# Two more pauses for the recurrence of a hybrid encoder layer, behind its wide sums and before its state

## The chip, the cores and the metric

The kernel runs on one core of a Trainium2 chip. A core has five engines with instruction queues of their own: TensorE (PE in the profile, its weight loads PEld), VectorE (DVE), ScalarE (ACT), GpSimd (POOL) and SyncE (SP), and sixteen DMA engines that serve all of them. The metric is the device time in microseconds of one execution; lower is better.

## The reference

One layer of an encoder for 512 positions of width 1024, in float32. It has three parts, each between two RMS norms and added to the residual:

```python
h = rmsnorm(x, pre_mix_g[l])
aq, ak, av, hq, hf_fwd, hf_bwd, hi, hg = split_columns(h @ w_in[l], IN_SPLITS)
...
att = axial_gqa_attention(apply_rope(aq, cos, sin), apply_rope(ak, cos, sin), av)
rec = hgrn2_group(hq, hf_fwd, hf_bwd, hi, hg, lb_all[:, l], hg_out_norm_g[l])
mixed = jnp.concatenate([att, rec], axis=-1) @ w_out[l]
x = x + rmsnorm(mixed, post_mix_g[l])
...
x = x + rmsnorm(memory_cross_attention(h, m, w_xq[l], w_xkv[l], w_xo[l]), post_x_g[l])
...
x = x + rmsnorm(conv_ffn(h, w_up[l], conv_w[l], conv_b[l], w_down[l]), post_ffn_g[l])
```

The attention has 8 heads of 64 with 2 key heads. The recurrence (`rec`) is a gated scan in both directions with 4 heads of 128: a state of keys by values decays by a gate at each position and takes in the new key and value. The cross-attention reads 256 memory rows, and the feed-forward part has 2816 columns.

## The kernel before

Every large product is made of three matmuls on split operands: each float32 operand is a rounded high part and a remainder, and `mm3` (lines 296 to 298) adds high by high, high by low and low by high in PSUM. Weights come in units of 128 x 1024 through `issue`: a load to `raw` on the SP queue, a cast to `wh` on ScalarE (L240), and the remainder `wl`, for some units by VectorE (L242), for others as a negated copy (L245 on GpSimd, L247 on ScalarE) to which a DMA of the GpSimd queue adds the weight (L248). `issue_ahead` starts units up to three ahead of their use (`AHEAD`).

The order of the instructions comes about in two steps. First, Python generators write the program: each stream of work is a generator that yields how many microseconds of work it has just written, and `weave` goes on with the stream that has the least of its total behind it. The sum of these steps is the planner's clock (`clock[0]`), which is a plan and not a time. `pace(us)` lets a stream yield nothing until the other streams have moved that clock on by `us`. A stream in `late` that pauses is put level with the next one, so that it does not catch up afterwards. Second, the framework's scheduler orders each engine's queue: of the instructions that its model holds to be ready, the one written first goes first. An instruction written later can so still run earlier, where an engine has nothing else.

The first weave runs two streams: `mix_projections` (total 100; the projections of the output gate, of the heads 1 to 3 of the recurrence, of the queries, keys and values) and `all_cores` (share 53, `CORE_SHARE`; the heads of the recurrence, one after another). A projection step is six matmuls of 512 columns and 1.296 of the planner's clock. The weave ends with the projections. The second weave takes what is left of the recurrence (share 34), `attention` (46; 32 steps and 3 to finish, 1.1 each) and `attention_filler` (52). The filler holds eight products for the memory's keys (half as wide, on PSUM bank `b`), four units for the first half of the memory's values, and the first half of the output product, `res_first`, whose order of weights is 0, 2, 3, 1: it starts when all four heads of the recurrence are written. Attention starts, after `ATT_LEAD`, when the keys are turned and the fourth head has begun (`begun[0] < 4`).

One head, `hgrn_core`, computes the scan without a loop over positions: products of gated keys and queries within pairs of blocks of 1, 2, 4, up to 64 positions fill the matrix `diag` by masks, level 128 fills its neighbour, and a state of keys by values carries between the halves of the sequence. In the heads 0 to 2 (`wide`) the first level is made in another way: two element products `near`, split into `sides`, are summed over the keys by a matrix of ones and zeros (`parity`, L722, "the wide sums"), and the result is copied to `diag` on ScalarE (L723). Then each level has two products in place on VectorE (L711), a copy of keys on ScalarE (L682), eight records of matmuls on bank `c` (L685) and a copy by mask on VectorE (L725). At the end the keys are turned on TensorE (L697), copied on ScalarE (L698), multiplied with the values into the state (L702, copied at L704), and the output follows (L731 to L733), with its norm, gate, a last turn (L749) and a split.

Before the change a wide head pauses at two places: `CORE_WIDE` (8.0) ahead of the wide sums, so that VectorE can make `sides`, and `CORE_END` (4.5) ahead of the gate.

In attention a step writes scores (L921, bank `s`), the softmax (reduction L899, exponent L902, reciprocal L903, scaling L907 on ScalarE or L909 on VectorE), and, two steps later, four turns (L931, bank `o`) with a split (L139 on ScalarE, L140 on VectorE); every fourth step also weighs the values (L942).

Of the kernel before, what the change touches and what calls it, by code (L numbers as in the profile page):

```python
# [47 lines left out]
NEG_SCALAR = frozenset(range(9, 33))  # L48
NEG_POOL = frozenset(range(33, 42))
CORE_SHARE, ATT_LEAD = 53.0, 4.0  # L50
CORE_WIDE, CORE_END = 8.0, 4.5
KEY_TURNS = {1: (0, 1), 2: (2, 3)}
WARM, SPREAD_STEP = 4, 2
LEVELS = (1, 2, 4, 8, 16, 32, 64)
# [5 lines left out]
def pat(t, off, dims):  # L60
    a = t[:]
    return bass.AP(tensor=a.tensor, offset=a.offset + off, ap=[list(a.ap[0])] + [list(d) for d in dims])
# [14 lines left out]
def pace(us):  # L77
    end = clock[0] + us
    while clock[0] < end and not stuck[0]:
        yield None  # L80
# [27 lines left out]
def layer(tc, io, out):  # L108
# [14 lines left out]
    def small():  # L123
        return sm.tile([P, 16], F32, name="small", tag="small")

    def bank(tag):
        return ps.tile([P, 512], F32, name="ps_" + tag, tag=tag)

    def big(shape, dt=F32):
        return b8.tile(shape, dt, name="big", tag="big")  # L130

    def tmp2(shape=(P, 512), dt=F32, tag="ta"):
        return t2.tile(list(shape), dt, name="tmp2", tag=tag, bufs=TMP_BUFS[tag])
# [4 lines left out]
    def split(hi, lo, src, eng=None):  # L138
        nc.scalar.copy(hi, src)  # L139
        (eng or nc.vector).tensor_sub(lo, src, hi.bitcast(F32))  # L140
# [159 lines left out]
    def blk(b):  # L300
        return slice(b * P, (b + 1) * P)
# [338 lines left out]
    def hgrn_core(h):  # L640
        while h not in heads:
            yield None
        q, qk, tt = heads[h]
        begun[0] += 1
        room = big([P, 2048])
        a = room[:, 0:1024].rearrange("p (s w n) -> p s w n", s=NB, w=2)
        kt = room[:, 1024:1536].rearrange("p (s n) -> p s n", s=NB)
        st = room[:, 1536:1792].rearrange("p (g n) -> p g n", g=2)
        diag = a[:, :, 0, :]
        wide = h < 3  # L650
        near = room[:, 1024:2048]
        ksum = tmp2(tag="th")
        nc.scalar.mul(ksum, qk[:, 1, 0, :], oml[:, 0, h:h + 1])
        if wide:
            nc.vector.tensor_tensor(out=pat(near, T, [[2, T // 2], [1 - T, 2]]), in0=pat(qk, 0, [[2, T // 2], [T + 1, 2]]),
                                    in1=pat(qk, 3 * T + 1, [[2, T // 2], [-(T + 1), 2]]), op=ALU.mult)
        nc.vector.scalar_tensor_tensor(out=ksum, in0=qk[:, 1, 1, :], scalar=oml[:, 1, h:h + 1], in1=ksum,
                                       op0=ALU.mult, op1=ALU.add)
        if wide:
            pairs = lambda t: t.rearrange("p (i two) -> p i two", two=2)  # L660
            nc.vector.tensor_tensor(out=pat(near, 0, [[2, T // 2], [T + 1, 2]]), in0=pairs(ksum), in1=pairs(q),
                                    op=ALU.mult)
            sides = [[tmp2(dt=F32R, tag="th") for _ in range(2)] for _ in range(2)]
            for n in range(2):
                split(*sides[n], near[:, n * T:n * T + T])
        else:
            kc, qc = [tmp2(tag="th") for _ in range(2)]
            for side, to in ((1, kc), (0, qc)):
                nc.scalar.copy(to, pat(qk, side * 2 * T, [[2, T // 2], [T + 1, 2]]))
            o = bank("c").rearrange("p (b n) -> p b n", b=NB)  # L670
            for b in range(NB):
                nc.tensor.matmul(o[:, b, :], ksum[:, blk(b)], q[:, blk(b)], start=True, stop=True)
            nc.scalar.copy(diag, o)
            yield 1.0
        toff = 0
        for i, m in enumerate(LEVELS + (128, 256)):
            if m == 1 and wide:
                pass
            elif m <= 64:
                if m > 1:  # L680
                    kc = tmp2(tag="th")
                    nc.scalar.copy(kc, pat(qk, 2 * T, [[2 * m, T // (2 * m)], [T + m, 2], [1, m]]))  # L682
                o = bank("c").rearrange("p (b n) -> p b n", b=NB)
                for b in range(NB):
                    nc.tensor.matmul(o[:, b, :], kc[:, blk(b)], qc[:, blk(b)] if m == 1 else  # L685
                                     pat(qk, b * P, [[2 * m, P // (2 * m)], [T + m, 2], [1, m]]),
                                     start=True, stop=True)
            elif m == 128:
                o = bank("c").rearrange("p (b n) -> p b n", b=NB)
                for sb in range(NB):  # L690
                    tb = sb ^ 1
                    nc.tensor.matmul(o[:, sb, :], qk[:, 1, sb % 2, blk(sb)], qk[:, 0, tb % 2, blk(tb)],
                                     start=True, stop=True)
            else:
                o = bank("c").rearrange("p (b n) -> p b n", b=NB)
                for sb in range(NB):
                    nc.tensor.transpose(o[:, sb, :], qk[:, 1, sb // 2, blk(sb)], ident)  # L697
                nc.scalar.copy(kt, o)  # L698
                yield 0.5
                o = bank("c")[:, :256].rearrange("p (g n) -> p g n", g=2)  # L700
                for sb in range(NB):
                    nc.tensor.matmul(o[:, sb // 2, :], kt[:, sb, :], v[:, sb, blk(h)],  # L702
                                     start=sb % 2 == 0, stop=sb % 2 == 1)
                nc.scalar.copy(st, o)  # L704
                yield 1.0
                break
            nblk = T // m
            npair = nblk // 2
            for s, off, gap in ((1, 1, nblk - 1), (0, nblk + 1, -(nblk + 1))):
                c = pat(qk, s * 2 * T, [[2 * m, npair], [T + m, 2], [1, m]])  # L710
                nc.vector.tensor_tensor(out=c, in0=c, in1=pat(tt, toff + off, [[2, npair], [gap, 2], [0, m]]),  # L711
                                        op=ALU.mult)
            if m < 128:
                src = tt[:, toff:toff + 2 * nblk].rearrange("p (i two) -> p two i", two=2)
                toff += 2 * nblk
                nc.vector.tensor_mul(tt[:, toff:toff + nblk], src[:, 0, :], src[:, 1, :])
                if m == 1 and wide:
                    yield from pace(CORE_WIDE)
                    o = bank("c")
                    for n in range(2):  # L720
                        for k in range(2):
                            nc.tensor.matmul(o, parity[:, n:n + P], sides[n][k], start=n + k == 0, stop=n + k == 2)  # L722
                    nc.scalar.copy(diag, o.rearrange("p (b n) -> p b n", b=NB))  # L723
                else:
                    nc.vector.copy_predicated(diag, masks[:, i:i + 1, :].to_broadcast([P, NB, P]), o)  # L725
            else:
                nc.scalar.copy(a[:, :, 1, :], o)
            yield 1.0
        o = bank("c").rearrange("p (b n) -> p b n", b=NB)
        for tb in range(NB):  # L730
            nc.tensor.matmul(o[:, tb, :], a[:, tb, 0, :], v[:, tb, blk(h)], start=True, stop=False)  # L731
            nc.tensor.matmul(o[:, tb, :], a[:, tb ^ 1, 1, :], v[:, tb ^ 1, blk(h)], start=False, stop=False)
            nc.tensor.matmul(o[:, tb, :], qk[:, 0, tb // 2, blk(tb)], st[:, 1 - tb // 2, :], start=False, stop=True)  # L733
        on = tmp2((P, NB, P), tag="th")
        ss = small()
        for b in range(NB):
            nc.scalar.activation(on[:, b, :], o[:, b, :], ACT.Square, accum_out=ss[:, b:b + 1])
        r = rstd_of(ss[:, :NB], NB, P)
        yield 3.0
        if wide:  # L740
            yield from pace(CORE_END)
        while len(sg_box) < 1 + NB:
            yield None
        for b in range(NB):
            nc.vector.scalar_tensor_tensor(out=on[:, b, :], in0=o[:, b, :], scalar=r[:, b:b + 1],
                                           in1=sg_box[0][:, b, blk(h)], op0=ALU.mult, op1=ALU.mult)
        o = bank("c").rearrange("p (b n) -> p b n", b=NB)
        for b in range(NB):
            nc.tensor.transpose(o[:, b, :], on[:, b, :], ident)  # L749
        if h % 2 == 0:  # L750
            pair(mix, 2 + h // 2)
        split_scaled(*mix.get(4 + h, slice(0, T)), o.rearrange("p b n -> p (b n)"), og[:, 0:1])
        rec_done[0] += 1
        yield 0.5
# [643 lines left out]
```

## Time and profile before

| | |
|---|---|
| median of 3 runs | 814.44 us (814.04 to 815.73) |
| profiled execution | 814.31 us, its span 812.5 us |
| mean granted TensorE clock | 0.998 |
| busy: TensorE, weight loads | 800.7 us, 688.4 us |
| busy: VectorE, ScalarE, GpSimd | 582.7, 482.0, 136.5 us |
| first and last wide sums (L722) | 55.8 and 168.3 us |
| first and last scores of attention (L921) | 208.5 and 299.0 us |

Times of rows are microseconds from the first instruction. TensorE's records overlap, since its matmuls are pipelined, so a busy TensorE need not run at its peak; its idle time is what no record covers. In the table of stretches each line gives the bounds and length of a stretch and then, for each engine, its busy time in it with the count of instructions, the granted clock, and the mean busy share of the DMA engines with GB/s. In the list of waits each line names the instruction that waited, what ended the wait, the total, the count and the longest. In the list of groups each line gives line, engine, operation, output and inputs with shapes and count, then busy time, mean ns of one, and the engine's idle time ahead of them.

### The profile page before, as it was taken

What the parts mean: (1) busy time and instruction counts of PE and PEld (TensorE: products, weight loads), DVE (VectorE), ACT (ScalarE), POOL (GpSimd) and SP (SyncE); (2) the same over time, 40 slices, a digit from 0 to 9 for tenths busy, and PEclk for the clock granted to TensorE, in tenths of its full rate; (3) what the DMA queues carried; (4) which work ended last, traced back from release to release, by engine and by line L of the source; (5) the groups of instructions that cost most, each with busy time, mean ns of one, the idle gap of its engine ahead of it and who ended that gap; (6) DMA issues with size and microseconds to landing.
All of it is one profiled execution on the core that took longest, in us unless ns stands there. A gap on an engine that the chain in (4) does not pass through costs nothing.

```text
span 812.5 us, 11696 instructions
## 1 busy us (share of the span) xinstructions
PE 800.7 (99%) x4390; PEld 688.4 (85%) x4390; DVE 582.7 (72%) x878; ACT 482.0 (59%) x797; POOL 136.5 (17%) x213
## 2 busy tenths in 40 slices
PE   9999999999999999999999999999999999999996
PEld 7888878899988888888888898899999998888885
DVE  5467576698896765855453767987777788888765
ACT  6675774677978873645443553665555545566651
POOL 0111201334213102301011311211111111000301
PEclk9999999999999999999999999999999999999999
DMA  8596666679777752256634158776765667278842
GB/s 300 198 267 164 137 148 130 146 187 267 206 193 191 186 188 109 86 173 170 167 117 143 33 165 205 161 199 164 187 166 141 160 187 179 91 211 277 241 127 104
DMA packets 42458, 139.61 MB, mean 172 GB/s; under 512 B 5281, under 2 KB 6561, under 8 KB 42401
## 3 DMA queue, kind: packets, MB, share of 16 engines
q1 hardware_dynamic: 28944, 97.43, 35.0%
q0 software_dynamic: 12160, 38.54, 26.8%
q10 hardware_dynamic: 1296, 2.89, 1.0%
q8 instruction: 34, 0.56, 0.3%
q14 instruction: 24, 0.19, 0.1%
HBM read 135.17 MB, written 25.17 MB: 197 GB/s over the span
## 4 chain that ended last, share of the span: by engine, by line
PE 89%; DVE 4%; ACT 4%; issue 1%; DMA 1%; POOL 1%; SPq 0%; DVEq 0%; POOLq 0%
PE ps_b L298 9%; PE ps_b L297 9%; PE ps_b L296 9%; PE ps_s L296 7%; PE ps_s L298 7%; PE ps_s L297 7%; PE ps_o L296 5%; PE ps_o L298 5%; PE ps_o L297 5%; PE ps_c L296 4%; PE ps_c L298 4%; PE ps_c L297 4%; PE ps_c L685 2%; PE ps_o L942 1%; PE ps_o L931 1%; PE ps_s L921 1%
## 5 line engine op out<-in xcount | busy, mean ns | idle before, releaser
L240 ACT CAST wh<-raw 128x1024 fp32r<-128x1024 f32 x110 | 113.8, 1036 | 106.9 <-PE ps_b L297 30.2
L242 DVE TENSOR_TENSOR wl<-raw,wh 128x1024 fp32r<-128x1024 f32 (+1 forms) x77 | 92.9, 1209 | 72.5 <-ACT wh L240 72.4
L296 PE MATMUL ps_b<-big,wh 128*128 128x512 f32 (+1 forms) x344 | 122.2, 355 | 0.0
L298 PE MATMUL ps_b<-big,wl 128*128 128x512 f32 (+1 forms) x344 | 120.9, 351 | 0.0
L297 PE MATMUL ps_b<-big,wh 128*128 128x512 f32 (+1 forms) x344 | 120.4, 350 | 0.0
L298 PEld LDWEIGHTS ps_b<-big,wl 128*128 128x128 f32 x344 | 65.0, 189 | 8.7
L297 PEld LDWEIGHTS ps_b<-big,wh 128*128 128x128 f32 x344 | 65.1, 189 | 8.2
L296 PEld LDWEIGHTS ps_b<-big,wh 128*128 128x128 f32 x344 | 65.1, 189 | 8.0
L711 DVE TENSOR_TENSOR big<-big 128x512 f32<-128x512 f32 x64 | 48.3, 769 | 9.2 <-ACT tmp L682 4.8
L296 PE MATMUL ps_s<-wh,big 128*128 128x512 f32 (+1 forms) x140 | 53.5, 383 | 0.1
L297 PE MATMUL ps_s<-wl,big 128*128 128x512 f32 (+1 forms) x140 | 53.2, 380 | 0.0
L298 PE MATMUL ps_s<-wh,big 128*128 128x512 f32 (+1 forms) x140 | 53.0, 379 | 0.0
L248 POOL DMA_DIRECT2D wl<-in_w_dram x33 | 29.4, 890 | 118.7 <-ACT wl L247 105.6
L140 DVE TENSOR_TENSOR big<-ps_o,big 128x512 fp32r<-128x512 f32 x54 | 36.8, 686 | 11.5 <-ACT big L139 11.3
L139 ACT CAST big<-ps_o 128x512 fp32r<-128x512 f32 x54 | 31.8, 589 | 17.0 <-PE ps_o L1047 7.5
L296 PE MATMUL ps_s<-big,wh 128*128 128x256 f32 (+1 forms) x120 | 40.0, 333 | 0.0
L297 PE MATMUL ps_s<-big,wh 128*128 128x256 f32 (+1 forms) x120 | 39.9, 333 | 0.0
L298 PE MATMUL ps_s<-big,wl 128*128 128x256 f32 (+1 forms) x120 | 39.9, 332 | 0.0
L297 PE MATMUL ps_c<-big,wh 128*128 128x256 f32 (+1 forms) x120 | 39.1, 325 | 0.0
L296 PE MATMUL ps_c<-big,wh 128*128 128x256 f32 (+1 forms) x120 | 39.1, 325 | 0.0
L298 PE MATMUL ps_c<-big,wl 128*128 128x256 f32 (+1 forms) x120 | 39.0, 325 | 0.0
L296 PE MATMUL ps_o<-wh,big 128*128 128x512 f32 (+1 forms) x102 | 38.8, 380 | 0.0
(322 smaller groups left out, 2147.1 us busy)
## 6 DMA issues: line engine op xcount, KB each, us to landing
raw<-in_w_dram SPq DMA_DIRECT2D x91, 512.0 KB, 3.4
wl<-in_w_dram POOLq DMA_DIRECT2D x33, 512.0 KB, 6.8
sum_t<-in_wd_dram SPq DMA_DIRECT2D x20, 512.0 KB, 6.0
tmp<-in_wu_dram SPq DMA_DIRECT2D x14, 512.0 KB, 7.3
sum_t<-in_wd_dram POOLq DMA_DIRECT2D x10, 512.0 KB, 8.1
sum_t<-sum_t POOLq DMA_DIRECT2D x10, 512.0 KB, 7.4
big<-sum_t SPq DMA_DIRECT2D x10, 512.0 KB, 4.9
raw<-sum_t SPq DMA_DIRECT2D x10, 512.0 KB, 3.8
```

The costliest lines, as they stand in the source:

```text
L139: nc.scalar.copy(hi, src)
L140: (eng or nc.vector).tensor_sub(lo, src, hi.bitcast(F32))
L240: nc.scalar.copy(wh, raw)
L242: last_low[0] = nc.vector.tensor_sub(wl[:, :by_dma], raw[:, :by_dma], wh[:, :by_dma].bitcast(F32)).ins
L248: nc.gpsimd.dma_start(wl[:, by_dma:], source(i)[:, by_dma:], accum_op=ALU.add)
L296: nc.tensor.matmul(o, a[0], b[0], start=start, stop=False, skip_group_check=again)
L297: nc.tensor.matmul(o, a[0], b[1], start=False, stop=False, skip_group_check=again)
L298: last_mm[0] = nc.tensor.matmul(o, a[1], b[0], start=False, stop=stop, skip_group_check=again).ins
L685: nc.tensor.matmul(o[:, b, :], kc[:, blk(b)], qc[:, blk(b)] if m == 1 else pat(qk, b * P, [[2 * m, P // (2 * m)], [T + m, 2], [1, m]]), st ...
L711: nc.vector.tensor_tensor(out=c, in0=c, in1=pat(tt, toff + off, [[2, npair], [gap, 2], [0, m]]), op=ALU.mult)
L921: nc.tensor.matmul(s, qT[h // 4][:, h % 4, blk(qb)], kT[:, 2 * (h // 4) + c, :], start=c == 0, stop=c == 1)
L931: nc.tensor.transpose(o[:, c, :], e[:, 0, blk(c)], ident)
```

## The change

Two pauses are added to `hgrn_core`. One stands behind the copy of the wide sums to `diag`, in the heads 0 to 2: the levels from 2 on are written only when the other streams have advanced the planner's clock by 4.0. The other stands, in all four heads, between the copy of the turned keys `kt` and the products that form the state, for 2.6. No instruction is added, removed or changed; only the order in which they are written.

```diff
-CORE_WIDE, CORE_END = 8.0, 4.5
+CORE_WIDE, CORE_SUMS, CORE_COPY, CORE_END = 8.0, 4.0, 2.6, 4.5
...
                 nc.scalar.copy(kt, o)
                 yield 0.5
+                yield from pace(CORE_COPY)
                 o = bank("c")[:, :256].rearrange("p (g n) -> p g n", g=2)
...
                     nc.scalar.copy(diag, o.rearrange("p (b n) -> p b n", b=NB))
+                    yield from pace(CORE_SUMS)
                 else:
```

## The prediction

> **What bounds the kernel now.** I read the page first, then who waits for whom on TensorE in the stages that hold the recurrence, then the chain at the two longest waits, then busy time by stretches. The profiled execution took 814.31 us (span 812.5, 1.8 around it), 0.13 under the median of 814.44. All sums are made against 814.31; 0.2% of it is 1.6 us, about what a measurement of this kernel can tell from no change, and the three chances below are cut there.
>
> ```profile
> PE 800.7 (99%) x4390; PEld 688.4 (85%) x4390; DVE 582.7 (72%) x878; ACT 482.0 (59%) x797; POOL 136.5 (17%) x213
> PE 89%; DVE 4%; ACT 4%; issue 1%; DMA 1%; POOL 1%; SPq 0%; DVEq 0%; POOLq 0%
> ```
>
> TensorE is the bound, and the change adds and removes no instruction. It can only move idle time of TensorE. What there is of it between 52 and 312 us, waiting engine first, then for whom, total, times, longest:
>
> ```profile
> PE ps_c L685 <- ACT tmp L682: 0.9, 1, 0.9
> PE ps_c L702 <- ACT big L698: 0.5, 1, 0.5
> PE ps_c L685 <- DVE big L711: 0.4, 1, 0.4
> PE ps_o L931 <- DVE big L140: 0.3, 1, 0.3
> PE ps_s L921 <- ACT tmp L902: 0.2, 1, 0.2
> PE ps_o L931 <- ACT tmp L907: 0.2, 1, 0.2
> ```
>
> The first two rows are the two places of the change; all six sum to 2.5 us, so perfection gives 811.8. The chain at each (start, duration, what):
>
> ```profile
> 110.74 0.96 ACT wl L247
> 111.70 0.47 ACT big L723
> 112.17 0.58 ACT tmp L682
> 112.79 1.23 PE ps_c L685 x8
> ...
> 193.58 1.05 ACT wh L240
> 194.63 0.27 ACT tmp L773
> 194.89 0.50 ACT big L698
> 195.44 1.16 PE ps_c L702 x8
> ```
>
> Head 1 (111 us): the copy of the wide sums sits on ScalarE behind a weight's pass, then the next level's key copy, and the products of that level wait for it. Head 2 (195 us): the copy of the turned keys sits behind two passes of other work, and the products that form the state wait. Heads 0 and 3 show neither wait.
>
> **The change part by part.** A pause is no instruction: it holds back where in program order the rest of the recurrence is written until the other stream has advanced the planner's clock by so much. The instruction order then follows from that order and readiness.
>
> *Wait behind the wide sums (4.0, heads 0 to 2) and before the state (2.6, all heads).* Projection steps are 1.296 on the planner's clock, so a pause ends at a whole step: four steps, 5.2, for 4.0; in these stages two or three for 2.6. A step is six 512-column products, in the trace 0.23 to 0.24 us each (rows "PE ps_b" below), 1.4 us. Either pause covers its wait several times over, and the covering products had to be done anyway, so cover costs nothing where the other stream has work. Gain: 0.9 + 0.5 = 1.4 us. Its ends are 0, if the late copy only moves behind another ScalarE pass, and 2.5, if all six rows go. I take 1.4. What is late next at 113 us is the level's two key products on VectorE, inside the same pause.
>
> *What is queued behind the pauses.* Nothing waits on the chip. But all later parts of the recurrence are written later, on ScalarE and VectorE too. I stepped both weaves through by hand with the yields of the code (projections 98.5 in all; one head 13.0, and 13.0 x 100/53 = 24.5 of projections beside it, plus its pauses). Heads 0, 1 and 2 began at 1.3, 51.9 and 102.5 of the planner's clock; with the change at 1.3, 59.7 and 118.0. The first weave ends with the projections: at 132.5 before (34 of recurrence written), at 124.5 after (26). So before, head 2 had only its turned keys, state and output left for the second weave; after, it enters it ahead of its wide sums. There is no catching up, since a pausing stream is put level with the other. Attention may start only when head 3 has begun: 154.2 before, 167.1 after. In the meantime the memory keys run out: the eighth is done at 184.9 before, 161.1 after. Head 3 ends at 205.5 before, between attention's steps 19 and 20; at 218.0 after, behind step 28. All is written by 245.8 in both.
>
> *What that does on the chip.* Attention is the part that eats ScalarE and VectorE, and it loses its filler. Busy time in the two halves of today's attention (span, then PE, PEld, DVE, ACT, POOL, clock, DMA share, GB/s), the reductions L899 (one a step) and the weight casts L240 in each:
>
> ```profile
> 208.00:266.00 58.00, 56.77 (x371) 49.09 (x370) 48.11 (x97) 49.07 (x104) 15.54 (x17) 1.00 0.79 200
> 266.00:308.00 42.00, 42.00 (x215) 34.17 (x214) 30.60 (x57) 31.31 (x63) 3.88 (x5) 1.00 0.69 205
> ...
> 208.00:266.00 58.00, 12.82 (x20) 1.00 0.79 200
> 266.00:308.00 42.00, 8.75 (x13) 1.00 0.69 205
> ...
> 208.00:266.00 58.00, 7.42 (x7) 1.00 0.79 200
> 266.00:308.00 42.00, 4.23 (x4) 1.00 0.69 205
> 208.00:229.00 21.00, 20.67 (x144) 18.19 (x143) 19.33 (x40) 20.28 (x43) 3.60 (x4) 1.00 0.80 202
> ```
>
> And TensorE's prices, from the chain (start, duration, what), the first row with attention's first scores:
>
> ```profile
> 208.71 0.92 PE ps_s L921 x4
> ...
> 248.42 1.91 PE ps_o L942 x8
> 250.79 0.89 PE ps_c L702 x8
> 251.68 0.46 PE ps_s L921 x2
> 252.14 0.44 PE ps_o L931 x4
> 252.58 0.23 PE ps_b L296
> 253.97 0.22 PE ps_c L731 x2
> ```
>
> One attention step on TensorE: 0.46 (scores) + 0.44 (turns) + 1.91/4 (weighing) = 1.38 us. On ScalarE, from the second half: 31.31 less 4.23 of weight casts and 1.9 for the head's last pass (L143) and two memory value casts (L139 on ps_b) is 25.2; between 13 scores and 15 turns (L899 above, L140 in the group row below) that is 14 steps, 1.80 us each. So a step is ScalarE's before it is TensorE's, and only other matmuls beside it keep TensorE full.
>
> ```profile
> L140 DVE TENSOR_TENSOR big<-ps_o,big 128x512 fp32r<-128x512 f32 x15 | 10.1, 686 | 2.3 <-ACT big L139 2.1
> L240 ACT CAST wh<-raw 128x1024 fp32r<-128x1024 f32 x4 | 4.2, 1058 | 0.6 <-issue 0.5
> L139 ACT CAST big<-ps_b 128x512 fp32r<-128x512 f32 x2 | 1.2, 600 | 0.0
> L143 ACT ACTIVATE big<-ps_c,og 128x512 fp32r<-128x512 f32 x1 | 0.7, 697 | 0.0
> L682 ACT COPY tmp<-big 128x512 f32<-128x512 f32 x6 | 3.9, 653 | 0.0
> L902 ACT ACT_TABLE_LOAD x1 | 1.3, 1283 | 0.4 <-DVE small L899 0.4
> ```
>
> After the change, up to head 3's end:
> ScalarE: 28 steps x 1.80 = 50.4; head 3's seven copies of 0.5 to 0.65 by the row and some eight smaller passes, 7.9 together (an estimate); three weight casts at 1.06, 3.2; the table load 1.3. Sum 62.8.
> TensorE: 28 x 1.38 = 38.6; head 3, nine groups at 0.89, twelve pairs at 0.22 and two turns at 0.44, 11.5; the five of eight memory-value steps still left by then, 5 x 1.4 = 7.0; of the output product, whose first halves are ready early, none to four steps, 0 to 5.6, middle 2.8. Sum 59.9.
> ScalarE reached 20.28/21 = 97% in attention's first 21 us, and 49.07/58 = 85% over the first half. By the first the stretch takes 64.7, by the second 73.9; at the mean of 91% 69.0. TensorE would idle 4.8, 14.0 or 9.1 of it. Today it idles 58 - 56.77 = 1.2 there. The 1.80 itself is generous: the first half, by the same sum (about 19 steps and seven casts), would come to 52 where 49.07 was measured, 6% less. With 6% off, 62.8 becomes 59.0 and the three idle times 0.9, 9.5 and 4.9. I take 4.9 - 1.2 = 3.7, rounded to 4; ends -0.3 (all filled) and +8.3, and the lower end goes to -1.2 if attention's own waits vanish too. VectorE, at 48.11 of 58 today, points the same way. Head 2's levels leave the stretch of q and k norms, but TensorE loses too little there to gain.
>
> *DMA.* Every weight is fetched by its use count, so key weights are asked for sooner. Eight key units lie 4.4 planned us apart (130.4 to 161.1), against 6.4 before. In the busiest stretch, 195 to 229 us (queue, packets, MB, share of 16 engines):
>
> ```profile
> q0 software_dynamic: 720, 2.62, 44.4%
> q1 hardware_dynamic: 1303, 4.47, 37.7%
> ...
> wl<-in_w_dram POOLq DMA_DIRECT2D x4, 512.0 KB, 7.8
> raw<-in_w_dram SPq DMA_DIRECT2D x3, 512.0 KB, 3.4
> ```
>
> Added, the queues filled 82% of 34 us for about four units, 7.0 us a unit. I count nothing here: three units are asked ahead, and a late key product leaves its matmuls for attention to lean on. No instruction of SP or POOL is added; only their times move. The Trainium skill, DMA: Bandwidth & Descriptors, section Issuing engines are not separate DMA queues, says that transfers from all issuing engines run on the same 16 engines and interleave; read so, the shares add as above, while with separate queues each would be under half full and this limit would not exist. The mean DMA share of 0.80 between 208 and 229 us agrees with adding.
>
> Sum: 814.31 - 1.4 + 4.0 = 816.9; on the median 817.0.
>
> The Trainium skill, Perfetto Trace Analysis, section Identifying the Most-Contended Engine, calls matmul busy time a poor measure and points to LDWEIGHTS busy; by its 85% some 124 us would be free for pauses to win. The trace disagrees: in 266 to 308 us LDWEIGHTS shows 34.17 of 42 while no wait of TensorE stands there.
>
> **The rivals.**
> *Absorbed: faster.* The scheduler pulls output and head 3 work forward, attention's stretch ends even, and both waits go. It decides if the stretch idles under 1 us: by the 97% row with 6% off, 0.9. Time 814.31 - 1.4 - 0.3 = 812.6; with all rows gone 811.8. For it: TensorE fell idle only 1.2 of 58 us with ScalarE at 85%. Against: filler then was 4 key units richer. Chance 0.28.
> *No change in effect.* The waits move to other levels, or the gain and a small squeeze cancel: 814.4 (812.8 to 816.0). For it: a copy can sit behind a weight's pass anywhere, and two heads show no wait at all. Chance 0.27.
> *Key weights late: slower.* From the first key (planned 124.5) to attention's start (167.1) 42.6 planned us, some 45 on the chip, eight units beyond the three asked ahead are due; at 7.0 us each they need 56, so TensorE, with 11 us short, stalls on the weights' low parts. With 4 us of that made up by attention written behind, 814.31 - 1.4 + 7 = 819.9. Against: the mean over calmer stretches is lower, and 45/8 = 5.6 us a unit is all it must hold. Chance 0.10.
> The forecast, squeeze in attention, has 0.35; own range 816 to 821.
>
> **How the numbers follow.** Faster 0.28 is the first rival; same 0.27 the second; slower 0.45 the forecast and the third. The time is the forecast's, 817.0. The low end is 811.8 (all six rows gone), the high end 821.5, above the late keys and just under the squeeze's upper end, 814.31 - 0 + 8.3 = 822.6.
>
> **What would show it.** The rows L685 <- L682 and L702 <- L698 of heads 1 and 2 gone: the gain. First scores (L921) near 219 instead of 208 us, the wide sums of head 2 behind the last projection: the move. TensorE idle, waiting for ACT L902, L907 or DVE L140, L899 in the 55 us after the first scores, some 5 us in all: the squeeze. Waits of L298 for the POOL queue or of L240 for its load near 200 to 215 us: the late keys. I am wrong if the attention stretch shows under 1 us of idle, or if the first scores stay near 208.

## The result, and the profile after

The changed kernel takes 826.65 us (median of 6 runs, 825.60 to 831.86) beside 815.03 us (814.04 to 816.36) for the kernel before in the same series: ratio 1.0151, 95% interval 1.0124 to 1.0179. It is slower, by some 12 us. The profiled execution took 825.60 us with a span of 823.8. Lines in the rows of the changed kernel are one or two higher than before: L712 was L711, L703 was L702, L723 was L722 (the wide sums, whose copy is now L724), L923 was L921; in e14, e16, e17 and e18 an edit moves them further.

The page, busy time of each engine after: the same matmuls in 11.3 us more of span. TensorE's busy time has grown with it, by 3.9 us.

```profile
PE 804.6 (98%) x4390; PEld 689.8 (84%) x4390; DVE 581.4 (71%) x878; ACT 482.4 (59%) x797; POOL 138.2 (17%) x213
```

Busy time thus hides part of the loss. In its place I use this: at a granted clock of 1.00 TensorE's records start 0.227 us apart at 512 columns, 0.120 at 256 and 0.110 at 128 when nothing holds them (medians of the trace); what a stretch lasts beyond the sum of these steps over the records started in it is called lost below. All losses are those of a kernel's one profiled execution, and for e3, e10 and e13 further down that was its longest, 2.1, 3.0 and 4.0 us above the median.

| us lost by TensorE in | 50 to 180 | 180 to 230 | 230 to 290 | 290 to 345 |
|---|---|---|---|---|
| before | 3.2 | 3.2 | 2.5 | 0.9 |
| after | 2.5 | 8.0 | 10.1 | 0.9 |

So 0.7 us is gained up to 180 us, 4.8 lost by 230 and 7.6 by 290; the sum, 11.7, is near the 11.3 by which the span grew. As idle time alone, 180 to 230 us has 4.9 where before had 0.9, and 230 to 290 us 5.1 where before had 0.9; the rest of the loss is records that start late without leaving a gap. The same stretches by engine (bounds, length, then PE, PEld, DVE, ACT, POOL, clock, DMA share, GB/s), before and then after:

```profile
180.00:230.00 50.00, 49.13 (x382) 46.02 (x382) 43.57 (x105) 44.46 (x92) 14.17 (x20) 1.00 0.84 216
230.00:290.00 60.00, 59.09 (x344) 49.60 (x343) 47.17 (x91) 47.44 (x101) 14.49 (x16) 1.00 0.77 198
...
183.00:208.00 25.00, 24.46 (x209) 23.94 (x209) 20.43 (x58) 20.19 (x43) 9.47 (x15) 1.00 0.94 243
208.00:230.00 22.00, 21.67 (x152) 19.19 (x151) 20.33 (x43) 21.28 (x44) 3.84 (x5) 1.00 0.77 193
```

```profile
180.00:230.00 50.00, 45.14 (x340) 41.34 (x339) 34.95 (x81) 33.04 (x64) 21.77 (x27) 1.00 1.02 283
230.00:290.00 60.00, 54.89 (x323) 44.51 (x322) 55.49 (x115) 54.11 (x115) 6.28 (x6) 1.00 0.45 119
...
183.00:208.00 25.00, 21.38 (x167) 19.73 (x167) 23.69 (x61) 17.25 (x32) 9.79 (x14) 1.00 1.04 296
208.00:230.00 22.00, 20.96 (x154) 19.02 (x153) 8.26 (x18) 12.99 (x27) 11.42 (x12) 1.00 1.01 266
267.00:290.00 23.00, 20.48 (x125) 16.57 (x125) 20.81 (x44) 20.29 (x46) 0.00 (x0) 1.00 0.00 1
```

Read the VectorE column downward. Before it is fairly even: 20.43 of 25 us, then 20.33 of 22. After it is 95% full up to 208 us, 38% full up to 230, and 92% full from 230 to 290. Work has been pushed into heaps, and ScalarE follows it. The DMA column has its own heap, 1.02 in 180 to 230, and is at 0.00 from 267 to 290: the next load of a weight is issued at 304 us. Products of weights, which could cover attention, have become few there. In that stretch the first of the three lines of `mm3` has these records, before and then after (all three lines: 53 records before, 4 after):

```profile
L296 PE MATMUL ps_b<-wh,big 128*128 128x512 f32 x11 | 4.7, 432 | 0.0
L296 PE MATMUL ps_c<-wh,big 128*128 128x512 f32 x6 | 2.6, 436 | 0.0
```

```profile
L296 PE MATMUL ps_b<-wh,big 128*128 128x512 f32 x2 | 1.0, 476 | 0.0
```

TensorE's waits between 52 and 325 us after (who waited, for whom, total, times, longest), to be set beside the six of the prediction:

```profile
PE ps_s L923 <- ACT tmp L904: 3.3, 3, 1.5
PE ps_s L807 <- ACT big L798: 1.5, 2, 0.8
PE ps_c L723 <- DVE tmp L140: 1.0, 2, 0.6
PE ps_o L933 <- DVE big L140: 0.8, 2, 0.5
PE ps_c L697 <- DVE big L712: 0.8, 1, 0.8
PE ps_b L297 <- DMA wl<-in_w_dram: 0.7, 1, 0.7
PE ps_c L685 <- DVE big L712: 0.6, 1, 0.6
PE ps_c L685 <- ACT tmp L682: 0.6, 1, 0.6
```

The first is attention's scores behind its own exponents, the second the turning of attention's keys behind ScalarE's copies of them; one transfer stands there, with 0.7 us. Attention's scores, in the row of that line (count, shortest, median and longest in ns, first and last start):

```profile
L923 PE MATMUL ps_s<-big x64: 387/396/500, 228.4 to 310.6; 128*128 128x512 f32 x64
```

They began at 228.4 instead of 208.5 us.

### The profile page after: what moved, and what is told of

Its sections match the earlier page's. It is cut to its first block, busy times and chain, and to the rows that moved or that the text cites. A ratio compares the mean times of both kernels' runs of the same rounds, so it can differ in the third digit from the quotient of the medians.

```text
span 823.8 us, 11701 instructions
## 1 busy us (share of the span) xinstructions
PE 804.6 (98%) x4390; PEld 689.8 (84%) x4390; DVE 581.4 (71%) x878; ACT 482.4 (59%) x797; POOL 138.2 (17%) x213
## 4 chain that ended last, share of the span: by engine, by line
PE 92%; DVE 4%; ACT 2%; DMA 1%; issue 1%; POOL 0%; DVEq 0%; POOLq 0%; ACTq 0%
PE ps_b L296 9%; PE ps_b L297 9%; PE ps_b L298 9%; PE ps_s L296 7%; PE ps_s L297 7%; PE ps_s L298 7%; PE ps_o L296 5%; PE ps_o L298 5%; PE ps_o L297 5%; PE ps_c L296 4%; PE ps_c L298 4%; PE ps_c L297 4%; PE ps_c L685 3%; PE ps_o L944 2%; PE ps_s L923 2%; PE ps_s L525 1%
## 5 line engine op out<-in xcount | busy, mean ns | idle before, releaser
L297 PE MATMUL ps_b<-big,wh 128*128 128x512 f32 (+1 forms) x344 | 120.6, 350 | 0.0
L297 PEld LDWEIGHTS ps_b<-big,wh 128*128 128x128 f32 x344 | 65.1, 189 | 7.9
L712 DVE TENSOR_TENSOR big<-big 128x512 f32<-128x512 f32 x64 | 47.5, 759 | 21.9 <-PE ps_c L685 10.4
L297 PE MATMUL ps_s<-wl,big 128*128 128x512 f32 (+1 forms) x140 | 53.0, 379 | 0.0
L140 DVE TENSOR_TENSOR big<-ps_o,big 128x512 fp32r<-128x512 f32 x54 | 37.0, 686 | 11.7 <-ACT big L139 11.7
L297 PE MATMUL ps_s<-big,wh 128*128 128x256 f32 (+1 forms) x120 | 39.9, 333 | 0.0
L297 PE MATMUL ps_c<-big,wh 128*128 128x256 f32 (+1 forms) x120 | 39.1, 326 | 0.0
```

The lines of the kernel that those rows point to most:

```text
L297: nc.tensor.matmul(o, a[0], b[1], start=False, stop=False, skip_group_check=again)
```

## The experiments

Two questions: is it the shift of everything written later, or the place of the pauses; and what makes the two lost stretches. The losses by stretch of all runs stand here once, with the mean granted clock in 180 to 230 and 230 to 290 us (last column: ratio to the kernel before, of the same series, with its interval).

| | 50 to 180 | 180 to 230 | 230 to 290 | 290 to 345 | clock | ratio |
|---|---|---|---|---|---|---|
| e1_sums | 3.4 | 8.6 | 9.7 | 1.6 | 0.97, 1.00 | 1.0179 (1.0163 to 1.0195) |
| e2_copy | 3.3 | 12.6 | 2.2 | 0.9 | 0.86, 1.00 | 1.0116 (1.0101 to 1.0131) |
| e3_shift | 2.9 | 9.4 | 24.0 | 6.9 | 0.93, 0.80 | 1.0377 (1.0348 to 1.0406) |
| e4_comp | 4.3 | 2.7 | 1.8 | 0.7 | 1.00, 1.00 | 1.0004 (0.9995 to 1.0014) |
| e5_seeds | 2.4 | 9.8 | 10.2 | 0.9 | 0.97, 1.00 | 1.0180 (1.0153 to 1.0206) |
| e6_gate3 | 2.4 | 7.7 | 5.5 | 0.9 | 0.97, 1.00 | 1.0079 (1.0065 to 1.0093) |
| e7_keys | 2.5 | 7.2 | 8.2 | 0.9 | 1.00, 1.00 | 1.0114 (1.0100 to 1.0128) |
| e8_neutral | 1.7 | 3.1 | 2.2 | 0.7 | 1.00, 1.00 | 0.9979 (0.9970 to 0.9988) |
| e9_share | 2.4 | 9.2 | 2.5 | 0.9 | 0.97, 1.00 | 1.0056 (1.0042 to 1.0070) |
| e10_turns | 2.3 | 10.9 | 10.3 | 1.4 | 0.98, 0.99 | 1.0154 (1.0137 to 1.0170) |
| e11_both | 2.5 | 7.0 | 2.5 | 0.9 | 1.00, 1.00 | 1.0040 (1.0026 to 1.0054) |
| e12_sums1 | 1.7 | 3.1 | 2.2 | 0.7 | 1.00, 1.00 | 0.9977 (0.9967 to 0.9986) |
| e13_plain_k | 4.5 | 8.5 | 10.9 | 1.3 | 0.95, 0.98 | 1.0135 (1.0120 to 1.0151) |
| e14_no_low | 3.0 | 9.5 | 10.3 | 0.9 | 0.97, 1.00 | 1.0162 (1.0148 to 1.0176) |
| e15_ends | 2.0 | 5.7 | 2.3 | 1.2 | 0.97, 1.00 | 1.0024 (1.0015 to 1.0034) |
| e16_two | 2.6 | 7.7 | 10.1 | 1.1 | 0.97, 1.00 | 1.0122 (1.0107 to 1.0137) |
| e17_two_share | 2.9 | 5.0 | 2.7 | 0.8 | 1.00, 1.00 | 1.0011 (1.0002 to 1.0021) |
| e18_before_two | 3.1 | 1.8 | 2.6 | 0.7 | 1.00, 1.00 | 0.9966 (0.9953 to 0.9979) |

The clock is a part of some losses. 0.97 over 50 us is one piece of 3.4 us at 0.50; in e16's, from 223.8 to 227.2 us, records of 512 columns start 0.43 us apart instead of 0.227. By these numbers such a piece makes up to half its length of the loss, an estimate: 1.7 us at 0.97, some 7 of e2's 12.6, 12 of e3's 24.0. Before and the changed kernel have none there.

### Place or shift

Each pause alone; no new pause but a delay by the old pause at a head's end, in the kernel before (head 3 begins at 171.3 of the planner's clock, with both new pauses at 166.1); and both new pauses with the delay taken out of the old ones.

```diff
e1_sums   -CORE_WIDE, CORE_SUMS, CORE_COPY, CORE_END = 8.0, 4.0, 2.6, 4.5
          +CORE_WIDE, CORE_SUMS, CORE_COPY, CORE_END = 8.0, 4.0, 0.0, 4.5
e2_copy   +CORE_WIDE, CORE_SUMS, CORE_COPY, CORE_END = 8.0, 0.0, 2.6, 4.5
e3_shift  -CORE_WIDE, CORE_END = 8.0, 4.5
          +CORE_WIDE, CORE_END = 8.0, 11.0
e4_comp   +CORE_WIDE, CORE_SUMS, CORE_COPY, CORE_END = 3.0, 4.0, 2.6, 2.0
```

> Only the pause of 4.0 behind the wide sums; the one before the state is 0. Theory S (the shift): the loss depends on how late the rest of the recurrence is written, not on where the pauses stand. In the planner's order attention's first step (167.1) and head 3's end (218.0, behind 29 steps of attention) are the same as with both pauses, so the 7.6 us that TensorE lost above before in 230 to 290 us stay; head 2's wide sums are written at 121.9 instead of 128.5, so of the 4.6 lost in 180 to 205 us up to half goes: 8 to 12 us over before. Rival P (the place): each pause has its own price at its place, so one of two gives about half, +6.

> Only the pause of 2.6 before the state; the one behind the wide sums is 0. Theory S: attention begins at 158.7 of the planner's clock (154.2 before, 167.1 with both), head 3 ends behind 23 steps of attention (20 and 29): +1 to +4 us over before. Rival P: about half of the whole loss, +6.

> The kernel before, without the two new pauses, with CORE_END 11.0 instead of 4.5, so that heads 1 to 3 begin at 58.4, 115.4 and 171.3 of the planner's clock (with both pauses 59.7, 118.0, 166.1; before 51.9, 102.5, 153.2). Theory S: the same loss without any of the new pauses, +8 to +14 us. Rival P: no more than the price of a longer pause where one stood already, within 2 us of before.

> Both new pauses kept at 4.0 and 2.6, with CORE_WIDE 3.0 and CORE_END 2.0, so that the heads begin at 51.9, 102.5 and 151.2 as before (51.9, 102.5, 153.2), attention at 152.2 and head 3 ends behind 20 steps, as before. Theory S: the loss goes, -2 to +3 us against before (the wide sums may now wait for their sides, since their pause is cut from 8 to 3). Rival P: the loss stays, +10 to +12.

The shift decides. With both new pauses in their places and the heads' starts brought back, e4 is at 814.67 us beside 814.61, and both stretches lose less than before. With no new pause and a somewhat greater delay, e3 is at 845.64 us, worse than the change itself. e4's stretches, to be compared with those of before above:

```profile
180.00:230.00 50.00, 48.43 (x386) 45.69 (x385) 43.54 (x102) 44.89 (x91) 14.84 (x20) 1.00 0.81 210
230.00:290.00 60.00, 59.83 (x353) 50.99 (x352) 46.87 (x94) 48.04 (x103) 14.46 (x16) 1.00 0.79 203
```

What e4 gains there it pays at the wide sums, whose own lead was cut from 8.0 to 3.0 (its longest wait of TensorE):

```profile
PE ps_c L723 <- DVE tmp L140: 1.3, 1, 1.3
```

The sizes were missed. Beside before, e1 is 14.7 us slower (8 to 12 expected by the shift), e2 9.4 (1 to 4) and e3 31.0 (8 to 14). Less what the pieces at a clock of 0.50 could cost, about 2, 7 and 17 us by the estimate above (e3 has 34 us of them in all), they stand at 13, 2.6 and 14.

The two halves are not parts of one sum. e1 alone (829.3 us) is no better than both pauses together, and e2 alone (823.99) loses 12.6 us before 230, much of it by its clock, and nothing more than before behind it. On the planner's clock e2 lets attention start at 158.7, with head 3 behind 23 of its steps; e1 and the change at 167.1, behind 29. In e1, e2, e4 and the change the stretch from 230 to 290 goes with that count, the one before it does not.

### The stretch from 230 to 290 us

Three edits of the changed kernel: attention may begin when head 2 has begun; the last three memory keys are held until head 3 has begun; the recurrence's share in the second weave goes from 34 to 45, so that head 3 is written after 21 steps of attention.

```diff
e6_gate3  -        while not turned[0] or begun[0] < 4:
          +        while not turned[0] or begun[0] < 3:
e7_keys   +            while c >= 5 and begun[0] < 4:
          +                yield None
e9_share  -    weave((cores, 34.0), (attention(), 46.0), (attention_filler(), 52.0))
          +    weave((cores, 45.0), (attention(), 46.0), (attention_filler(), 52.0))
```

> The kernel with both pauses; attention may begin when the third head has begun, not the fourth. In the planner's order its first step comes at 143.6 instead of 167.1, 13 steps stand ahead of the last key (none with both pauses, 13 before), and head 3's end stays where it was, at 218.0 behind 29 steps. Theory F (filler): TensorE's loss in attention comes from its filler being used up; it falls from 7.6 above before to under 3, and keys asked for more slowly cut the other loss too: 0 to +5 over before. Rival O (order): the loss comes from head 3 standing behind 29 steps instead of 20; it stays, +8 to +12.

> The kernel with both pauses; the memory keys 5 to 7 are written only when head 3 has begun. That cuts short head 2's pauses (its state at 150.0 instead of 153.8), attention begins at 155.5 instead of 167.1, and 13 of its steps stand ahead of the last key, at 175.4 or so, with head 3's end again at 218.0 behind 29 steps. Theory F: +0 to +5 over before, the loss in attention under 3. Rival O: +8 to +12.

> The kernel with both pauses; the recurrence's share in the second weave is 45 instead of 34. In the planner's order head 2's wide sums stay at 128.5 in the second weave, but attention begins at 161.9 with 13 steps ahead of the last key, and head 3 ends behind 21 steps (20 before, 29 with both pauses). Theory: the loss has two parts, 4.6 us in 180 to 205 us (head 2's levels meeting the last keys' norms and turns) and 7.6 in 230 to 290 us (attention without filler and the output product held behind head 3). This undoes the second alone: the loss there falls to about that of before, 2 to 4 us, the first stays: +4 to +6 over before. Rival: everything hangs on head 2's start, 118.0 instead of 102.5; the whole stays, +10 to +12.

e9 ends the loss of this stretch (2.5 us, as before) without a word changed in attention or the pauses: 818.95 us. e6 halves it (5.5), with attention beside the keys but head 3 still late, 6.7 us over before, between the ranges of its two readings (0 to 5 and 8 to 12). If the two effects add, which no run tests, some 4.6 us of the 7.6 belong to attention without filler and about 3 to head 3, and the output product behind it, coming late. e7 missed: I had expected the held keys to fill the stretch to under 3 us, and it kept 8.2; its 9.0 us over before is what the rival, the order, gave. Three half-wide products seem too little beside the 29 steps; no run shows it by itself. e9's row; TensorE stays full at the same load of VectorE and ScalarE (54.55 and 52.99 of 60) that left 5 us idle after the change, since matmuls lie beside them:

```profile
230.00:290.00 60.00, 59.62 (x350) 50.00 (x349) 54.55 (x110) 52.99 (x116) 10.88 (x12) 1.00 0.55 139
```

### The stretch from 180 to 230 us

Here the keys and queries of attention are normed, rotated and turned, head 2 goes through its levels and the memory's keys are made. What holds TensorE could be the transfers (a share of 1.02) or the queues of VectorE and ScalarE. First: the loads that nothing waits for (`SEEDS_AT`) ten units later in the order, which thins the traffic; the turns two steps later; the turns with e9's share; the keys' norm and rotation left out (a scaling in their place); the low parts' adding transfers left out for twelve units.

```diff
e5_seeds    -SEEDS_AT = frozenset(range(28, 46)) | frozenset(range(60, 66))
            +SEEDS_AT = frozenset(range(38, 56)) | frozenset(range(60, 66))
e10_turns   -KEY_TURNS = {1: (0, 1), 2: (2, 3)}
            +KEY_TURNS = {3: (0, 1), 4: (2, 3)}
e11_both    e9_share and e10_turns together
e13_plain_k -        kr = norm_rope(z[:, 0:128], 2, 1, b)
            +        kr = tmp2()[:, :128].rearrange("p (h d) -> p h d", h=2)
            +        nc.vector.tensor_scalar(kr, z[:, 0:128].rearrange(...), r[:, b:b + 1], None, op0=ALU.mult)
e14_no_low  +            if i not in range(26, 38):
                             nc.gpsimd.dma_start(wl[:, by_dma:], source(i)[:, by_dma:], accum_op=ALU.add)
```

> The kernel with both pauses; the copies within DRAM that are issued beside the weight units 28 to 45 (half a MB read and written each, for the sums of the last weights) go with the units 38 to 55, so that the key units 26 to 33 and the first value units have the DMA engines for weights alone. Theory D: what TensorE loses in 180 to 205 us (5.9 against 1.3 before, while the DMA engines were 1.04 full) is the key weights coming late; it falls to about 2, and the whole to +7 to +9 over before. Rival V: it is VectorE and ScalarE, on which head 2's levels meet the last keys' norms and turns; the loss stays, +11 to +13.

> The kernel with both pauses; the attention's keys are turned behind the memory keys 3 and 4 instead of 1 and 2 (145.9 and 150.0 of the planner's clock instead of 137.7 and 142.3). With both pauses TensorE lost some 2.2 us at the turns L807, waiting for casts and remainders of the keys. Theory V: those go and nothing else changes, since attention begins at 167.1 as it did: 1 to 3 us less than with both pauses, +9 to +11 over before. Rival: VectorE and ScalarE are full there, so the wait only moves to the next thing that they make: +11 to +13.

> Share 45 and the later turns together, with both pauses: if the two parts add, the gains of the two single edits add too: +2 to +4 over before. If the key stretch only moves its waits: as with the share alone, +4 to +6.

> The kernel with both pauses; the norm and the rotation of the attention's keys are left out (one scaling by the row's factor in their place), which takes some ten passes of VectorE, ScalarE and GpSimd per block out of 183 to 200 us. Theory V: what TensorE loses in 180 to 230 us above before (8.0 against 3.2) comes from VectorE and ScalarE having head 2's levels and the keys' norms at once; it falls to 3 to 5, the whole to +7 to +9. Rival D: it comes from the key weights and the casts that wait for their loads in ScalarE's queue; it stays within 1 us, +10.5 to +12.5.

> The kernel with both pauses; for the units 26 to 37 (memory keys, first memory values) the adding transfer of the low part is left out, which takes six MB of twelve off the DMA engines' weights there and the slowest step out of a unit's way. Theory V: nothing waits for the low parts on the whole, the loss in 180 to 230 us stays within 1 us of 8.0; the whole +10 to +12.5 (attention's part unchanged). Rival D: the loss there falls to 3 to 5, the whole to +7 to +9.

None of the four single edits brought the time below 826 us; by the ratios the best, e13, is 1.3 us better than the change, and the intervals overlap. The thinned traffic of e5 and e14, in the row of 183 to 208 us, leaves VectorE as full as after the change (first e5, then e14):

```profile
183.00:208.00 25.00, 21.98 (x157) 20.16 (x158) 23.02 (x58) 17.31 (x31) 9.90 (x14) 0.93 0.87 205
```

```profile
183.00:208.00 25.00, 21.98 (x169) 20.10 (x169) 24.39 (x60) 17.96 (x32) 5.03 (x9) 1.00 0.58 200
```

At a DMA share of 0.58 the loss is 9.5 us, or 7.8 less what its clock could cost, beside the 8.0 of the change. So transfers alone do not make it. Both runs came out slower than expected even for a loss that stays, 14.2 and 13.3 us over before (11 to 13 and 10 to 12.5). In e13 the loss up to 205 us falls from 5.9 to 3.2, but by 230 another 5.3 come on top (the change: 2.1). Up to 2.4 of them are its clock's, and a transfer does stand in the way:

```profile
PE ps_b L297 <- DMA wl<-in_w_dram: 1.7, 1, 1.7
PE ps_b L296 <- DVE big L140: 0.8, 1, 0.8
```

e1 shows the same limit bare, with 4.1 us in one wait (its list of waits, 180 to 235 us, and then its chain: the transfer that was waited for took 8.30 us):

```profile
PE ps_b L297 <- DMA wl<-in_w_dram: 4.1, 1, 4.1
```

```profile
214.95 1.03 POOL wl L245
215.98 0.28 issue
216.28 8.30 DMA wl<-in_w_dram
```

e10 only moved the wait (10.9 us lost, 3.1 of them in one wait for such a transfer), and with e9's share it helped by 1.3 us (e11; by the two ratios, whose intervals overlap). That left two readings open: two limits close behind one another, or an order that lacks ready work whoever serves it. The last three runs relieve both at once: in the changed kernel, in the changed kernel with the share of 45, and in the kernel before as a control.

```diff
e16_two         after:  the edits of e13_plain_k and e14_no_low
e17_two_share   after:  the same and (cores, 45.0)
e18_before_two  before: the edits of e13_plain_k and e14_no_low
```

> Both single reliefs at once in the changed kernel: the keys' norm and rotation are left out (a plain scaling stands in their place), and the adding transfer of the low parts is left out for the weight units 26 to 37. Taken singly, each left the loss of TensorE in 180 to 230 us at 8.5 to 9.5 us, the one with 1.7 us of waits for a weight's transfer, the other with waits for ScalarE's and VectorE's splits. Theory two limits (the queues of ScalarE and VectorE and the transfers stand close behind one another, and relieving one shows the other): the loss in 180 to 230 falls to 3 to 5 us, the stretch 230 to 290 keeps 9 to 11, the time is 820 to 823 us. Theory order (the delayed recurrence itself lacks ready work there, whatever serves it): the loss stays at 7 to 9, the time at 825 to 828.

> The same, and the recurrence's share in the second weave is raised from 34 to 45, which brought the stretch 230 to 290 back to 2.5 us of loss by itself. The same parts are left out. Theory two limits: both stretches near those of the kernel before, 3 to 5 and 2 to 3, time 813 to 816 us. Theory order: 180 to 230 keeps 7 to 9, time 817 to 820.

> The control: the same two parts left out of the kernel before. By every theory the stretches lose about what they lose in the kernel before or less (3.2 and 2.5 us), time 812.5 to 814.6 us; what the two runs of the changed kernel lose beyond this one is the shift's own.

e16 is at 825.29 us and the control at 812.35: the shift costs 12.9 us with both reliefs, 11.6 without them, as the order expected (825 to 828; two limits 820 to 823). In 180 to 230 us it costs 7.7 - 1.8 = 5.9 us, up to 1.7 of them by e16's clock, beside 4.8 without the reliefs. e17 came out the other way, inside what two limits had expected: 815.99 us (813 to 816) and 5.0 us lost (3 to 5; order 7 to 9). But the control gains from the reliefs too, and beside it e17 is 3.6 us slower, where e9 is 4.3 slower than before. So in both pairs the reliefs take little off the cost of the shift: the order fits best. Two limits are not excluded as a smaller part, since VectorE stayed 92% full in e16. The control's stretch and e16's show what remains:

```profile
183.00:208.00 25.00, 24.97 (x214) 24.54 (x214) 17.91 (x43) 20.11 (x40) 2.26 (x3) 1.00 0.50 165
208.00:230.00 22.00, 21.80 (x155) 19.42 (x153) 21.16 (x44) 20.88 (x44) 2.13 (x2) 1.00 0.28 98
```

```profile
183.00:208.00 25.00, 23.28 (x187) 22.13 (x188) 22.89 (x49) 18.74 (x31) 1.32 (x2) 1.00 0.58 200
208.00:230.00 22.00, 19.98 (x136) 18.02 (x135) 7.84 (x14) 10.91 (x23) 7.28 (x8) 0.92 0.65 219
```

VectorE is 92% full up to 208 us in e16 and 72% in the control, with the same key work left out. The difference is head 2's levels: products and masked copies number 10 and 3 in the control, 16 and 6 in e16. Before and after show the same in the groups of that stretch (line, operation, shape, count, then busy us and mean ns); first before, of whose products the last two are already head 3's, then after:

```profile
L711 DVE TENSOR_TENSOR big<-big 128x512 f32<-128x512 f32 x10 | 7.5, 775 | 0.1
L725 DVE COPY_PREDICATED big<-masks,ps_c 128x512 f32<-128x512 uint8 x4 | 2.9, 728 | 0.0
```

```profile
L712 DVE TENSOR_TENSOR big<-big 128x512 f32<-128x512 f32 x15 | 11.7, 798 | 0.6 <-PE ps_c L692 0.2 <-ACT tmp L682 0.2
L727 DVE COPY_PREDICATED big<-masks,ps_c 128x512 f32<-128x512 uint8 x6 | 4.4, 729 | 0.0
```

Five products and two masked copies more, 5.7 us of VectorE, stand in the 25 us in which queries and keys are prepared. Behind 208 us it has little to do, since attention waits for head 3; and there its order can cost TensorE once more. The changed kernel's chain (start, duration, what):

```profile
219.01 1.04 POOL small L315
220.07 0.87 DVE tmp L747 x3
...
222.30 2.15 DVE big L712 x2
224.45 0.27 DVE big L140
...
224.76 0.50 PE ps_b L296
```

The 0.27 us split of a memory key's product (L140) sits in VectorE's queue behind head 3's first two level products; bank `b` is free only after it. In the changed kernel this is a short wait:

```profile
PE ps_b L296 <- DVE big L140: 0.3, 1, 0.3
```

e14 and e16 have it with 2.1 and 2.0 us (`L297` behind `L140`), with no transfer in it. Of the change's 4.8 us, 4.6 are lost up to 205 us (5.9 beside 1.3 before) and 0.2 behind, so there the first of the two places counts. That it is head 2's levels is read from the queues: no run takes them alone out of the stretch.

### What a placed pause is worth

Pauses only where before showed a wait, with the starts of heads 2 and 3 kept by shortening heads 0 and 1 at their ends; the same without the pause ahead of the state; and the shortened ends alone.

```diff
e8_neutral -                yield from pace(CORE_COPY)
           +                yield from pace(CORE_COPY if h == 2 else 0.0)
           -                    yield from pace(CORE_SUMS)
           +                    yield from pace(CORE_SUMS if h == 1 else 0.0)
           -            yield from pace(CORE_END)
           +            yield from pace((0.0, 1.0, 4.5)[h])
e12_sums1  as e8_neutral, with pace(0.0) ahead of the state
e15_ends   as e12_sums1, with pace(0.0) behind the wide sums too
```

> Each new pause only where TensorE waited before: 4.0 behind the wide sums of head 1, 2.6 ahead of the state of head 2; the pause ahead of the gate is 0, 1.0 and 4.5 in the heads 0 to 2, so that head 2 begins at 102.5 and head 3 at 153.2 and attention at 154.2, all as before. If the two waits are worth what the trace shows and the shift is all that costs: 0.9 and 0.5 gone, -0.5 to -2 us. If the waits only move to another copy: within 0.5 of before.

> As the kernel with each pause only where TensorE waited before and the heads begun at the old places (2.05 us faster than before), but without the pause ahead of head 2's state. There the wait L703 for L698 stood at 0.5 us with the pause as it did without. If the gain is all from the wide sums of head 1: again 1.5 to 2.5 us faster than before. If the pause ahead of the state did its part: 0.5 to 1.2 us faster.

> The kernel before with the pauses ahead of the gate at 0, 1.0 and 4.5 instead of 4.5 each, and none of the new pauses: the control for the two kernels that are 2 us faster than before. Head 2 begins at 97.3 and head 3 at 142.8 of the planner's clock, head 3 ends behind 14 steps of attention. If the gain there is the pause behind head 1's wide sums: no gain here, -0.5 to +2 us. If it is the shorter pauses ahead of the gates: 1 to 2 us faster.

e8 takes 812.28 us and e12 812.60, beside 814.33 and 814.63 in their series: both beat the kernel before by 2.0 us, and the pause ahead of the state adds nothing that can be told. e15 is 2.2 us slower than before, so shorter ends alone gain nothing on the whole. But it also begins heads 2 and 3 earlier (97.3 and 142.8 of the planner's clock instead of 102.5 and 153.2), and its loss is in 180 to 230 us. Up to 180 us it loses 2.0, near e12's 1.7, and head 1's wait is gone there too, without any pause. What is shown is that the one pause, with the starts kept, makes an order that is 2.0 us faster; how much of it the place of the pause does stays open. e12's waits of TensorE between 52 and 340 us:

```profile
PE ps_c L703 <- ACT big L698: 0.5, 1, 0.5
PE ps_c L685 <- DVE big L712: 0.4, 1, 0.4
PE ps_o L933 <- DVE big L140: 0.3, 1, 0.3
PE ps_s L923 <- ACT tmp L904: 0.2, 1, 0.2
```

The wait behind ScalarE's copy of keys in head 1 is gone. The 0.5 us ahead of the state stands here and in e8 alike, where the pause is in place: it was not bought by that pause. e12 is the version to keep.

## Why the prediction was wrong in size

*Direction and mechanism: right.* The forecast was slower by a squeeze in attention, because all later work is written later while nothing catches up. e4 shows that this, and not the pauses themselves, makes the time, and e3 fits it.

*The squeeze, +4 taken between -0.3 and +8.3: mis-sized.* It measured +7.6 us (10.1 against 2.5 lost in 230 to 290), near the upper end. The failing step is the discount: 6% off the ScalarE sum, because the kernel before had done better than 1.80 us a step. The stretch that was priced, from attention's first scores to head 3's last turn, shows it:

```profile
228.40:298.50 70.10, 64.99 (x377) 52.67 (x375) 63.25 (x131) 62.99 (x139) 8.63 (x10) 1.00 0.41 110
```

ScalarE was busy 62.99 us, 90% of 70.1; the sum without the discount had 62.8 at 91%, 69.0 us, with it 59.0 and 64.8. By steps TensorE lost 10.2 us there, where the sum had 9.1 without and 4.9 with the discount. Two slips beside it are small or hidden: the sum has 28 attention steps where 29 are written (numbers 0 to 28), and it takes off 1.2 us of idle time for before, where by steps before lost 4.3. As idle time alone this stretch has 5.1 beside 1.2, 3.9 more; that this is the +4 is luck, since the sum did not price idle time. The list of waits named the engines rightly: scores behind the exponents (3.3 us) and turns behind VectorE's splits.

*"I count nothing here" for the keys' stretch: wrong, +4.8 us.* I looked for a cost there only in transfers. With a share of 1.02 they did fill up, as the added shares said they would, and one wait of 0.7 us is theirs; but e14 takes the share to 0.58 and the loss stays. What the runs show instead is the order of the queues (e16 beside its control), and the sentence that failed is the one on "the stretch of q and k norms": head 2's levels do not leave it. They fall into it, 15 products between 183 and 208 us where before had 8 of head 2's and 2 of head 3's.

*The rival of late keys as an alternative: wrong in form.* It was priced at 7 us in place of the squeeze. A loss among the keys and the squeeze lie in different stretches and add: 4.8 + 7.6. Late transfers as the cause are seen in e1, e10 and e13, where they held TensorE for 4.1, 3.1 and 1.7 us, and hardly in the change itself.

*The gain, 1.4: half.* Up to 180 us 0.7 was gained (3.2 to 2.5 lost). The wait of head 1 for its key copy went (as it did in e15, without a pause), but the wide sums there now wait 0.5 us for a split on VectorE (one of the two in the row L723 <- L140). The wait of head 2 ahead of the state is gone too, though one of 0.6 us for its key copy is new (L685 <- L682), and e8, with the pause in its place and the order kept, still has the one ahead of the state at 0.5 us: it is not the pause that removes it.

*First scores near 219: they came at 228.4 us.* On the planner's clock attention's start moved by 12.9 and on the chip by 20. The 4.8 us lost before them account for a part; the rest was not taken apart.

## What to carry to other kernels

A pause in a schedule of streams delays everything written behind it, so price the new order of the stages, not the wait that it removes: here the forecast gain was 1.4 us and the change cost 11.6. If a pause is placed, give the time back at the same stream's other pauses, and check that the later stages keep their start on the planner's clock (e4, e12); both a later and an earlier start cost (e3 and e15). When a stage is squeezed, look at every stretch that the work moves into, by each in-order queue, and add the losses instead of letting the forecasts compete. Before a run's loss is laid to a queue or a transfer, read the granted clock of the same stretch.

## What the runs showed of the hardware

The granted TensorE clock fell between 180 and 290 us in eleven of the eighteen runs (the column of the clock), and not only behind a long wait. In e1 the 4.1 us of one wait stand ahead of it; in e2 no wait was long. There it stood at 0.50 from 195 to 205 us (bounds, length, PE, PEld, DVE, ACT, POOL, clock, DMA share, GB/s):

```profile
190.00:195.00 5.00, 2.76 (x16) 2.00 (x16) 4.93 (x16) 5.00 (x12) 3.41 (x6) 0.89 1.02 337
195.00:200.00 5.00, 3.71 (x17) 3.55 (x18) 4.85 (x13) 2.28 (x6) 2.30 (x3) 0.50 1.06 256
200.00:205.00 5.00, 4.22 (x22) 3.92 (x20) 3.39 (x8) 1.07 (x2) 0.00 (x0) 0.50 0.80 188
```

Its longest wait of TensorE between 183 and 212 us:

```profile
PE ps_c L685 <- ACT tmp L682: 1.2, 1, 1.2
```

In the 5 us ahead TensorE was busy 2.76, in many short pieces. The Trainium skill, TensorE: Matmul & The Clock Gate, section HAM oscillation — how this bites in real kernels, ties the slow clock to idle gaps of more than about 3.4 us. This run shows it after a cluster of shorter ones, so a squeezed stretch can lose twice. In e2 that is up to some 7 of its 12.6 us; in the changed kernel itself the clock stayed at 1.00 in all stretches shown.
